# Down projection of a SwiGLU feed-forward layer: 16 of 22 depth tiles as seven half-width products

## The chip, the cores and the metric

The kernel runs on one core of one Trainium2 chip. The metric is the time of one execution on the device in microseconds. TensorE is the matrix engine, VectorE, ScalarE and GpSimd are the elementwise engines, SyncE issues the DMAs. In the profile they appear as PE (with PEld for its weight loads), DVE, ACT, POOL and SP.

## What is computed

The reference is one layer of a diffusion backbone: 512 latent tokens of width 1024 go through token mixers, then through a SwiGLU feed-forward layer of hidden width 2816 (22 tiles of 128), then through a final RMS norm. The change touches the end:

```python
def swiglu(h, w_gate, w_up, w_down):
    return (jax.nn.silu(h @ w_gate) * (h @ w_up)) @ w_down

# in reference():
h_lat = modulate(rms_norm(x, norm2_g[l]), mod_lat[3], mod_lat[4])
x = x + mod_lat[5] * swiglu(h_lat, ffn_w_gate[l], ffn_w_up[l], ffn_w_down[l])
...
return rms_norm(x, final_g)
```

`mod_lat[5]`, the gate of the residual, is one of six 1024-wide chunks of a projection of the conditioning vector.

## The kernel before

Everything lies transposed: a tile has 128 channels on its partitions and 512 tokens along its free axis. A product of weights and activations is done to nearly float32 accuracy by three matmuls: both operands are split into a rounded part `hi` and a rest `lo` (`split`, lines 128 to 130, and `load_unit`, lines 116 to 126: the cast on ScalarE, the subtraction on VectorE), and `mm3` (lines 132 to 137) adds hi x hi, hi x lo and lo x hi.

The feed-forward layer runs in two stages. In the gate and up stage each of 22 hidden tiles takes a gate and an up product of eight depth tiles. Four pairs are plain (`plain_pair`), 18 use `fast_pair` (lines 1094 to 1164): gate and up weights and the two token halves are the two-by-two blocks of a product that is formed from seven instead of eight half-width block products (Winograd's variant of Strassen's scheme). For that, VectorE makes four sums of weights for each pair (lines 1108 to 1112, `sa` and `sb`), and the sums of token halves are made once for the stage (`token_sums`). The seven products `p1` to `p7` have 12 matmuls each, of 256 columns. They come in two groups, `head` and `tail`: the tail of a pair is woven into the head of the next. Matmuls go in the order p1, p5 of the pair before, p7, p4 before, p6, p3 before, p2.

The down stage is plain: the 22 hidden tiles are split (loop over `hs`, lines 1187 to 1199, partly already during the gate and up stage), and each of eight output tiles takes three weight loads and 66 matmuls of 512 columns. `residual` (line 958) multiplies by the gate and adds into `x1`; squares are summed for the final norm. `ada(1)` loads one row block of the conditioning projection per output tile and makes a gate column from it on VectorE (line 861). The last output tile runs in two halves of 256 tokens, so that the norm and output of the first half run under the products of the second.

Raw weights pass through three buffers `wr` (`load_raw`, line 113), split ones through three pairs `whi` and `wlo`; within the fast pairs the split sums take four pairs `shi` and `slo`, the raw sums two buffers `S`. The order of the instructions on each engine is set ahead of time by a list scheduler from the program's order and its priorities (`tc.high_priority()` puts an instruction forward); at run time each engine works through its own queue in order. GpSimd's queue has memsets and eight elementwise products (line 795), all of them long before the feed-forward layer.

Of the kernel before, what the change touches and what calls it, by code (L numbers as in the profile page):

```python
# [12 lines left out]
P = 128  # L13
T = 512
# [38 lines left out]
def hybrid_block(ctx, tc, x, cx, cck, cc, wad, wada, vec, prm, cst, inv, win, wdt, wcv, wpl, wso, wout, wgu, wdn, out):  # L53
    nc = tc.nc

    class Ordered:
        def __init__(self, engine):
            self.engine = engine
# [31 lines left out]
    def vc(field, i, n=1):  # L90
        o = VEC_OFF[field] + i
        return vec_t[:, o : o + n]
# [856 lines left out]
    def project(o, ws, rhs, sl):  # L949
        n = sum(kn for _, kn in ws)  # L950
        q = 0
        for w, kn in ws:
            for k in range(kn):
                mm3(o[:, sl], w, k * P, tuple(a[:, sl] for a in rhs[q]), q == 0, q == n - 1)
                q += 1

    def residual(m, o, gate, base, sl, q, ms=None):
        V.scalar_tensor_tensor(x1[:, m, sl], o[:, sl], gate, base[:, sl], ALU.mult, ALU.add)
        if ms is None:
            sq_acc(acc[:, sl], x1[:, m, sl], m == 0, sl.stop - sl.start, q)  # L960
        else:
            S.activation(q[:, sl], x1[:, m, sl], AF.Square)
            PE.matmul(ms, mean, q[:, sl], start=False, stop=True)
# [80 lines left out]
    hid = []  # L1044

    def plain(u):
        if u < 3:
# [21 lines left out]
    def quad(tag, bufs, dt=F32):  # L1069
        return pt(f2, [P, 4, H], tag, bufs, dt)  # L1070
# [116 lines left out]
    hs = []  # L1187
    for q in range(NFF // 2):
        tags = ("shi", "slo") if q < 4 else ("T", "T") if q < 8 else ("S", "S") if q < 9 else None
        if tags:  # L1190
            pair = [pt(f2, [P, 2, T], tag, {"T": 8, "S": 2}.get(tag, 4), F32R) for tag in tags]
        for e in range(2):
            if tags:
                hi, lo = (a[:, e, :] for a in pair)
            else:
                hi, lo = (pt(per, [P, T], "hh", 8, F32R) for _ in range(2))
            split(hi, lo, hid[2 * q + e])
            hs.append((hi, lo))
    hid = hs

    acc = pt(per, [P, T], "sum", 1)
    for m in range(8):
        ada(1)
        o = mmp()
        ws = [(load_unit(wdn[m, :, k0 * P : (k0 + kn) * P], kn * P), kn) for k0, kn in ((0, 8), (8, 8), (16, 6))]
        for sl in halves if m == 7 else whole:
            ms = rms_head(sl) if m == 7 else None
            project(o, ws, hid, sl)
            residual(m, o, mod_l[:, 40 + m : 41 + m], x1[:, m, :], sl, pt(per, [P, T], "hl", 8), ms)
            S.activation(x1[:, m, sl], x1[:, m, sl], AF.Copy, scale=fin_n[:, m : m + 1])  # L1210
            if m < 7:
                continue
            rms_tail(ms, sl)
            n = T // 2
            for q in range(4):
                ot = pt(f2, [P, 2, n], "hid", NFF)
# [117 lines left out]
```

## Time and profile before

| | us |
|---|---|
| median of 3 runs | 976.66 (975.93 to 978.1) |
| profiled execution | 976.52 |
| its span, first to last instruction | 974.7 |
| TensorE busy in the span | 948.8 (97%) |
| VectorE busy | 764.9 (78%) |
| ScalarE busy | 492.2 (50%) |
| GpSimd busy | 15.9 (2%) |

The granted clock of TensorE is 0.996 of full speed over the span. The gate and up stage's fast pairs run from about 649 to 831 us, the down stage from 842 to 965, and the rest of 9.7 us is the second half's norm and output. A matmul's duration in the profile is longer than the distance to the next one, because matmuls overlap; what one costs is read from the distances.

### The profile page before, as it was taken

The page shows a single profiled execution, that of the slowest core. Times are in us where ns is not written, and L with a number is a line of the kernel's source. Part 1 is how long each engine was busy: PE and PEld are TensorE (multiplying, and loading weights), DVE is VectorE, ACT ScalarE, POOL GpSimd, SP SyncE. Part 2 cuts the span into 40 slices and gives each one's busy share as a digit, 9 for nine tenths or more (in the row PEclk, how much of TensorE's full clock was granted, in tenths as well). Part 3 has the DMA queues.
Part 4 walks back from the last instruction along what each step waited for, and adds up shares of the span by engine and source line. Part 5 has one row for each costly group of instructions (what it writes and reads, how often), then busy time and mean ns, then how long its engine had stood idle before and what let it go on. Part 6 is the DMA issues. An engine that isn't in the chain of part 4 may idle for free.

```text
span 974.7 us, 14173 instructions
## 1 busy us (share of the span) xinstructions
PE 948.8 (97%) x5420; PEld 803.6 (82%) x5420; DVE 764.9 (78%) x1165; ACT 492.2 (50%) x815; POOL 15.9 (2%) x58
## 2 busy tenths in 40 slices
PE   6999999999999999999999989999999999999996
PEld 4678888888887776777888769989999999888885
DVE  5589999967889999987876976999889888643333
ACT  5683597335445254644844434745555556432331
POOL 0000000000000000000000000000000000000000
PEclk9999999999999999999999999999999999999998
DMA  9753455321112346665578984223232323343422
GB/s 364 282 187 110 164 179 173 109 87 65 67 65 76 108 162 195 216 205 196 176 259 318 363 278 170 91 104 131 101 117 87 119 99 122 127 141 109 136 79 87
DMA packets 55492, 151.67 MB, mean 156 GB/s; under 512 B 5760, under 2 KB 16512, under 8 KB 54272
## 3 DMA queue, kind: packets, MB, share of 16 engines
q1 hardware_dynamic: 55424, 150.77, 44.6%
q8 instruction: 42, 0.69, 0.3%
q14 instruction: 26, 0.21, 0.1%
HBM read 134.43 MB, written 16.32 MB: 155 GB/s over the span
## 4 chain that ended last, share of the span: by engine, by line
PE 86%; DVE 7%; DMA 4%; ACT 2%; issue 1%; SPq 0%; DVEq 0%; ACTq 0%
PE mm L137 19%; PE mm L135 19%; PE mm L136 19%; PE mm L1122 10%; PE ps L1122 8%; PE mm L62 1%; DMA C<-mrg 1%; DVE wlo L123 1%; DVE A L403 1%; PE ps L1039 1%; PE ps L763 1%; PE y L825 1%; PE ps L62 1%; PE ps L715 1%; DMA wr<-in_wso_dram 1%
## 5 line engine op out<-in xcount | busy, mean ns | idle before, releaser
L135 PE MATMUL mm<-hh,whi 128*128 128x512 f32 (+1 forms) x612 | 242.4, 396 | 0.0
L137 PE MATMUL mm<-hh,wlo 128*128 128x512 f32 (+1 forms) x612 | 241.2, 394 | 0.5 <-DVE wlo L123 0.5
L136 PE MATMUL mm<-hl,whi 128*128 128x512 f32 x576 | 228.9, 397 | 0.0
L121 ACT CAST whi<-wr 128x1024 fp32r<-128x1024 f32 (+1 forms) x115 | 116.9, 1019 | 212.1 <-PE mm L136 167.4
L123 DVE TENSOR_TENSOR wlo<-wr,whi 128x1024 fp32r<-128x1024 f32 (+1 forms) x112 | 132.2, 1183 | 63.1 <-ACT whi L121 62.0
L137 PEld LDWEIGHTS mm<-hh,wlo 128*128 128x128 f32 x612 | 115.0, 188 | 28.3 <-issue 2.8
L135 PEld LDWEIGHTS mm<-hh,whi 128*128 128x128 f32 x612 | 115.1, 188 | 26.0 <-issue 1.7
L136 PEld LDWEIGHTS mm<-hl,whi 128*128 128x128 f32 x576 | 108.3, 188 | 25.0 <-issue 2.7
L403 DVE SCALAR_TENSOR_TENSOR A<-U,vec_t,A 128x504 f32<-128x504 f32 (+14 forms) x180 | 115.4, 684 | 0.1
L129 ACT CAST shi<-S 128x1024 fp32r<-128x1024 f32 x36 | 37.9, 1052 | 32.1 <-DVE S L1110 26.3
L1122 PE MATMUL mm<-T,shi 128*128 128x256 f32 x288 | 53.5, 283 | 0.0
L669 DVE SCALAR_TENSOR_TENSOR C<-C,vec_t,C 128x772 f32<-128x772 f32 (+1 forms) x48 | 46.9, 977 | 4.9 <-ACT C L667 2.4
L130 DVE TENSOR_TENSOR slo<-S,shi 128x1024 fp32r<-128x1024 f32 x36 | 44.1, 1225 | 5.8 <-ACT shi L129 5.7
L818 ACT ACTIVATE E<-E,sbias 128x128 f32<-128x128 f32 x128 | 40.0, 392 | 10.6 <-DMA E<-cumd 10.5
L1122 PEld LDWEIGHTS mm<-T,shi 128*128 128x128 f32 x288 | 44.8, 191 | 0.0
L129 ACT CAST whi<-wr 128x1024 fp32r<-128x1024 f32 (+1 forms) x36 | 30.0, 835 | 26.0 <-PE ps L1122 21.4
L861 DVE CUSTOM_DVE_ANT_0 wr<-wr,sil,vec_t 128x1024 f32<-128x1024 f32 x24 | 30.8, 1282 | 13.4 <-DMA wr<-in_wada_dram 13.4
L137 PE MATMUL mm<-H,wlo 128*128 128x256 f32 (+1 forms) x124 | 38.0, 307 | 2.9 <-DVE wlo L123 2.8
L1122 PE MATMUL mm<-T,slo 128*128 128x256 f32 x144 | 40.8, 284 | 0.0
L130 DVE TENSOR_TENSOR wlo<-wr,whi 128x1024 fp32r<-128x1024 f32 (+1 forms) x36 | 34.5, 958 | 7.6 <-ACT whi L129 6.0
L135 PE MATMUL mm<-H,whi 128*128 128x256 f32 (+1 forms) x124 | 37.8, 305 | 0.0
L136 PE MATMUL mm<-H,whi 128*128 128x256 f32 (+1 forms) x124 | 37.7, 304 | 0.0
(383 smaller groups left out, 2039.4 us busy)
## 6 DMA issues: line engine op xcount, KB each, us to landing
wr<-in_win_dram SPq DMA_DIRECT2D x62, 512.0 KB, 3.7
wr<-in_wgu_dram SPq DMA_DIRECT2D x44, 512.0 KB, 3.4
wr<-in_wada_dram SPq DMA_DIRECT2D x32, 512.0 KB, 4.0
E<-cumd SPq DMA_DIRECT2D x16, 512.0 KB, 5.3
wr<-in_wdn_dram SPq DMA_DIRECT2D x16, 512.0 KB, 3.9
X<-in_wad_dram SPq DMA_DIRECT2D x4, 1024.0 KB, 10.6
H<-in_wad_dram SPq DMA_DIRECT2D x4, 1024.0 KB, 11.2
mrg<-tmp SPq DMA_DIRECT2D x16, 256.0 KB, 4.0
```

What stands on the lines that cost most here:

```text
L121: S.copy(hi[:, :n], raw[:, :n])
L123: V.tensor_tensor(lo[:, :n], raw[:, :n], hi[:, :n], ALU.subtract)
L129: S.copy(dst_hi, src)
L130: V.tensor_tensor(dst_lo, src, dst_hi, ALU.subtract)
L135: PE.matmul(o, hi[:, col : col + P], rh, start=first, stop=False)
L136: PE.matmul(o, hi[:, col : col + P], rl, start=False, stop=False)
L137: PE.matmul(o, lo[:, col : col + P], rh, start=False, stop=last)
L403: V.scalar_tensor_tensor(accs[e][:, :, o], ins[e][:, :, q], vc("dw_w", (2 * j + e) * 31 + 15 + d), accs[e][:, :, o], ALU.mult, ALU.add)
L669: tap = V.scalar_tensor_tensor(a[:, 0:n], pad[:, k : n + k], vc("conv_w", i * 5 + k), a[:, 0:n], ALU.mult, ALU.add)
L818: S.activation(dec[d][:, j, :], dec[d][:, j, :], AF.Identity, bias=sbias[:, z, c : c + 1])
L861: V.tensor_tensor_reduce(raw, raw, silb[0], 1.0, vc("b_ada", i), ALU.mult, ALU.add, mod_l[:, i : i + 1])
L1122: PE.matmul(o[:, left], x[:, cs], rhs[k][y], start=first and k + n == 0, stop=k == 3 and n == 2, skip_group_check=True,)
```

## The change

The hidden tiles are kept in pairs. The first six of the 22 depth tiles are multiplied plainly: eight output tiles of 18 matmuls. The other 16 form two blocks of eight depth tiles. In a block, two output tiles (in the place of gate and up) and two token halves take the seven products of the fast pairs. Block 0 does all four pairs of output tiles, block 1 the first three; output tiles 6 and 7 of block 1 are plain, 24 matmuls each, tile 7 in two halves as before. Three contributions instead of one are added into `x1`. Each product leaves PSUM on its own: three by ScalarE with the gate as scale (`take`), four by VectorE with the gate and `x1` (`put`). GpSimd adds the first three into `x1` and makes the weight sums and the token sums. The gate columns are loaded and made during the six plain depth tiles, one for each output tile.

```diff
     def gated(up, sg):
-        h = pt(f2, [P, T], "hid", NFF)
+        if len(hid) % 2 == 0:
+            pairs.append(pt(f2, [P, 2, T], "hid", NFF // 2 + 1))
+        h = pairs[-1][:, len(hid) % 2, :]
         V.tensor_tensor(h, up, sg, ALU.mult)
...
-    adas.extend((5, q) for q in range(8))
+    gate_raw = deque()
+    def gate_load(m):
+        gate_raw.append(load_raw(wada[24 + m], 1024))
+    def gate_product(m):
+        raw, i = gate_raw.popleft(), 40 + m
+        V.tensor_tensor_reduce(raw, raw, silb[0], 1.0, vc("b_ada", i), ALU.mult, ALU.add, mod_l[:, i : i + 1])
...
+    gate_load(0)
     for i in range(NFF - PLAIN_TAIL, NFF):
         plain_pair(i)
...
+    KR = NFF - 16
+    down = []
+    for q in range(KR // 2):
+        hi, lo = (pt(f2, [P, 2, T], tag, 4, F32R) for tag in ("shi", "slo"))
+        split(hi, lo, pairs[q])
...
+    class Block:
...
+        def split_tile(self, hi, lo, sl):
+            k = len(self.x)
+            split(hi[:, sl], lo[:, sl], self.raw[k // 2][:, k % 2, sl])
+            self.x.append((hi, lo))
+        def token_sums(self):
+            for q in range(2):
+                a, b = (self.raw[q][:, :, sl] for sl in (left, right))
+                c, d = (self.raw[q + 2][:, :, sl] for sl in (left, right))
+                for dst, x, y in ((a, b, a), (b, d, b), (d, d, a), (c, c, d)):
+                    nc.gpsimd.tensor_tensor(dst, x, y, ALU.subtract)
+        def split_sum(self, n):
+            hi, lo = quad("T", 8, F32R), quad("T", 8, F32R)
+            base, sl = {1: (0, left), 3: (0, right), 2: (2, right), 4: (2, left)}[n]
+            for q in range(2):
+                es = slice(2 * q, 2 * q + 2)
+                split(hi[:, es, :], lo[:, es, :], self.raw[base + q][:, :, sl])
...
+    def down_pair(blk, j):
+        ks = slice(blk.k0 * P, (blk.k0 + 8) * P)
+        g, u = (load_raw(wdn[2 * j + e, :, ks], 1024) for e in range(2))
...
+        pool = nc.gpsimd.tensor_tensor
+        wa = parts(g, 1024)
+        pool(sa[:, c[0]], g[:, c[0]], u[:, c[0]], ALU.subtract)
+        pool(sb[:, c[0]], u[:, c[0]], u[:, c[1]], ALU.add)
+        pool(sa[:, c[1]], sb[:, c[0]], g[:, c[0]], ALU.subtract)
+        ws = parts(sa, 1024, 1)
+        pool(sb[:, c[1]], g[:, c[1]], sa[:, c[1]], ALU.subtract)
+        wu = parts(u[:, c[1]], T)
+        wt = parts(sb, 1024, 1)
...
+        def take(dst, o, gate):
+            with tc.high_priority():
+                S.activation(dst, o[:, left], AF.Copy, scale=gate)
+        def put(dst, o, gate):
+            with tc.high_priority():
+                V.scalar_tensor_tensor(dst, o[:, left], gate, dst, ALU.mult, ALU.add)
...
+        def p2():
+            product(b3, wa, T, blk.half(4, left), True)
+            put(x0[:, left], b3, g0)
+            pool(x0[:, left], x0[:, left], gt[:, left], ALU.add)
+            pool(x1u, x1u, ut, ALU.add)
+        def p5():
+            product(b1, wt, 0, blk.d[1], False)
+            put(x1u[:, right], b1, u0)
...
+        return (p1, p7, p6, p2), (p5, p4, p3)
...
     for m in range(8):
-        ada(1)
+        w = load_unit(wdn[m, :, 0 : KR * P], KR * P)
+        if m < 7:
+            gate_load(m + 1)
         o = mmp()
-        ws = [(load_unit(wdn[m, :, k0 * P : (k0 + kn) * P], kn * P), kn) for k0, kn in ((0, 8), (8, 8), (16, 6))]
+        project(o, [(w, KR)], down, whole[0])
+        gate_product(m)
+        add_down(m, o, whole[0])
+        if m in (2, 3, 4, 5):
+            b0.split_sum((3, 2, 1, 4)[m - 2])
+    jobs = [(b0, j) for j in range(4)] + [(b1, j) for j in range(3)]
+    tail = ()
+    for n, (blk, j) in enumerate(jobs):
+        head, nxt = down_pair(blk, j)
+        if n == 4:
+            b1.split_sum(3)
+            b1.split_sum(2)
+        for i in range(4):
+            head[i]()
+            if i < len(tail):
+                tail[i]()
+                if n == 4 and i < 2:
+                    b1.split_sum((1, 4)[i])
+        tail = nxt
+        if n < 3:
+            for _ in range((3, 3, 2)[n]):
+                a = pt(f2, [P, 2, T], "hid", NFF // 2 + 1, F32R)
+                b1.split_tile(a[:, 0, :], a[:, 1, :], whole[0])
+            if n == 2:
+                b1.token_sums()
+    ws = [load_unit(wdn[m, :, b1.k0 * P :]) for m in (6, 7)]
+    for f in tail:
+        f()
+    for m in (6, 7):
+        o = mmp()
         for sl in halves if m == 7 else whole:
             ms = rms_head(sl) if m == 7 else None
-            project(o, ws, hid, sl)
-            residual(m, o, mod_l[:, 40 + m : 41 + m], x1[:, m, :], sl, pt(per, [P, T], "hl", 8), ms)
-            S.activation(x1[:, m, sl], x1[:, m, sl], AF.Copy, scale=fin_n[:, m : m + 1])
+            project(o, [(ws[m - 6], 8)], b1.x, sl)
+            add_down(m, o, sl)
+            done(m, sl, ms)
```

`done` squares an output tile for the final norm and scales it, as before; `add_down` is the add from PSUM with the gate; `parts` splits a raw operand as in `fast_pair`.

## Rows read from the trace of the kernel before

**Rows 1.** Busy time by stretch: fast pairs, down stage (us, instructions; clock, DMA).

```profile
core 0: us, PE busy (x) PEld busy (x) DVE busy (x) ACT busy (x) POOL busy (x), PEclk, DMA share, GB/s
706.61:806.68 100.07, 100.07 (x843) 100.07 (x842) 86.07 (x121) 54.32 (x91) 0.00 (x0) 1.00 0.30 106
842.20:965.00 122.80, 122.65 (x600) 103.22 (x598) 45.63 (x57) 33.92 (x41) 0.00 (x0) 1.00 0.35 112
```

**Rows 2.** Chain of waits: start, duration (us), what; job starts, then successive output tiles.

```profile
706.61 2.86 PE mm L1122 x24
...
716.62 2.86 PE mm L1122 x24
...
736.63 2.86 PE mm L1122 x24
...
869.31 0.23 PE mm L135
...
884.37 0.24 PE mm L135
```

**Rows 3.** Timeline of VectorE, last output tile: start, duration (us), instruction, [idle before].

```profile
955.89 0.48 DVE L958 SCALAR_TENSOR_TENSOR X<-mm,mod_l,X 128x256 f32<-128x256 f32 x1 [6.29 <-PE mm L137]
...
960.56 2.50 DVE L1217 TENSOR_TENSOR hid<-X,sum 128x512 f32<-128x512 f32 x4
965.04 0.48 DVE L958 SCALAR_TENSOR_TENSOR X<-mm,mod_l,X 128x256 f32<-128x256 f32 x1 [1.98 <-PE mm L137]
967.27 0.43 DVE L143 TENSOR_TENSOR tmp<-tmp 128x256 f32<-128x256 f32 x1 [1.75 <-ACT tmp L141]
...
968.64 2.50 DVE L1217 TENSOR_TENSOR hid<-X,sum 128x512 f32<-128x512 f32 x4
```

**Rows 4.** Timeline of VectorE in the fast pairs, back-to-back instructions.

```profile
734.52 1.22 DVE L130 TENSOR_TENSOR wlo<-wr,whi 128x1024 fp32r<-128x1024 f32 x1
735.65 1.22 DVE L130 TENSOR_TENSOR slo<-S,shi 128x1024 fp32r<-128x1024 f32 x1
736.79 0.68 DVE L1055 TENSOR_TENSOR hid<-tmp,tmp 128x512 f32<-128x512 f32 x1
737.39 0.41 DVE L1145 TENSOR_TENSOR tmp<-tmp,ps 128x256 f32<-128x256 f32 x1
737.72 0.68 DVE L130 TENSOR_TENSOR wlo<-wr,whi 128x512 fp32r<-128x512 f32 x1
```

**Rows 5.** Instructions of one line: durations in ns (min/median/max), first and last start.

```profile
L795 POOL TENSOR_TENSOR W<-X,cbd x8: 1046/1158/2025, 326.9 to 445.2; 128x512 f32<-128x512 f32 x8
...
L820 DVE COPY_PREDICATED E<-msk,E x8: 1350/1390/2229, 130.1 to 427.0; 128x1024 f32<-128x1024 int32 x8
...
L403 DVE SCALAR_TENSOR_TENSOR A<-U,vec_t,A x4: 716/720/1511, 326.7 to 329.4; 128x488 f32<-128x488 f32 x4
```

**Rows 6.** Timeline of GpSimd and VectorE where a GpSimd product runs.

```profile
326.93 1.40 POOL L795 TENSOR_TENSOR W<-X,cbd 128x512 f32<-128x512 f32 x1 [37.37 <-DVE cbd L791]
...
353.33 1.27 POOL L795 TENSOR_TENSOR W<-X,cbd 128x512 f32<-128x512 f32 x1 [25.00 <-DVE cbd L791]
...
353.61 2.23 DVE L820 COPY_PREDICATED E<-msk,E 128x1024 f32<-128x1024 int32 x1
...
384.12 1.38 DVE L820 COPY_PREDICATED E<-msk,E 128x1024 f32<-128x1024 int32 x1
384.33 2.02 POOL L795 TENSOR_TENSOR W<-X,cbd 128x512 f32<-128x512 f32 x1 [29.73 <-issue]
```

**Rows 7.** Groups of VectorE in the down stage: count, busy us, mean ns, idle before.

```profile
L861 DVE CUSTOM_DVE_ANT_0 wr<-wr,sil_f,vec_t 128x1024 f32<-128x1024 f32 x6 | 7.7, 1285 | 21.6 <-DMA wr<-in_wada_dram 21.6
L123 DVE TENSOR_TENSOR wlo<-wr,whi 128x768 fp32r<-128x768 f32 x8 | 7.6, 950 | 0.0
L958 DVE SCALAR_TENSOR_TENSOR X<-mm,mod_l,X 128x512 f32<-128x512 f32 x7 | 5.3, 750 | 10.6 <-PE mm L137 10.6
...
L958 DVE SCALAR_TENSOR_TENSOR X<-mm,mod_l,X 128x256 f32<-128x256 f32 x2 | 1.0, 484 | 8.3 <-PE mm L137 8.3
```

**Rows 8.** DMA issues of the down stage: count, KB each, median us to landing.

```profile
wr<-in_wada_dram SPq DMA_DIRECT2D x7, 512.0 KB, 3.5
```

More of the change, by code (lines that the diff above doesn't have):

```diff
@@ L1042, in hybrid_block @@
                 PE.matmul(o[:, sl], lo[:, k * P : (k + 1) * P], h2[k][0][:, sl], start=False, stop=k == KT - 1)
-    hid = []
+    hid, pairs = [], []
     def plain(u):
@@ L1183, in hybrid_block @@
         f()
+    gate_load(0)
     for i in range(NFF - PLAIN_TAIL, NFF):
         plain_pair(i)
[L1187 to L1194, printed above, removed]
-            else:
-                hi, lo = (pt(per, [P, T], "hh", 8, F32R) for _ in range(2))
-            split(hi, lo, hid[2 * q + e])
-            hs.append((hi, lo))
@@ L1199, in hybrid_block, with __init__, half @@
-    hid = hs
-    acc = pt(per, [P, T], "sum", 1)
+    KR = NFF - 16
[3 more added lines that the diff above has]
+        split(hi, lo, pairs[q])
+        down += [(hi[:, e, :], lo[:, e, :]) for e in range(2)]
+    class Block:
+        def __init__(self, n):
+            self.k0 = KR + 8 * n
+            self.raw = pairs[self.k0 // 2 : self.k0 // 2 + 4]
+            self.x, self.d = [], {}
+        def split_tile(self, hi, lo, sl):
[14 more added lines that the diff above has]
+                split(hi[:, es, :], lo[:, es, :], self.raw[base + q][:, :, sl])
+            self.d[n] = [(hi[:, k, :], lo[:, k, :]) for k in range(4)]
+        def half(self, k0, sl):
+            return [tuple(a[:, sl] for a in self.x[k0 + k]) for k in range(4)]
@@ new lines, in down_pair, with parts, product, p1 @@
+    def down_pair(blk, j):
+        ks = slice(blk.k0 * P, (blk.k0 + 8) * P)
+        g, u = (load_raw(wdn[2 * j + e, :, ks], 1024) for e in range(2))
+        g0, u0 = (mod_l[:, 40 + 2 * j + e : 41 + 2 * j + e] for e in range(2))
+        x0, x1u = (x1[:, 2 * j + e, :] for e in range(2))
+        c = slice(0, T), slice(T, 2 * T)
+        sa, sb = pt(f2, [P, 2 * T], "S", 2), pt(f2, [P, 2 * T], "S", 2)
+        def parts(src, n, tag=None):
+            if tag is None:
+                hi, lo = pt(per, [P, 1024], "whi", 3, F32R), pt(per, [P, 1024], "wlo", 3, F32R)
+            else:
+                hi, lo = pt(f2, [P, 1024], "shi", 4, F32R), pt(f2, [P, 1024], "slo", 4, F32R)
+            split(hi[:, :n], lo[:, :n], src)
+            return hi, lo
+        pool = nc.gpsimd.tensor_tensor
[7 more added lines that the diff above has]
+        wt = parts(sb, 1024, 1)
+        b1, b2, b3 = mmp(), psp(), psp()
+        gt, ut = tmp(), tmp()
+        def product(o, w, base, rhs, first):
+            for k in range(4):
+                cs = slice(base + k * P, base + (k + 1) * P)
+                for n, (x, y) in enumerate(((w[0], 0), (w[0], 1), (w[1], 0))):
+                    PE.matmul(
+                        o[:, left], x[:, cs], rhs[k][y],
+                        start=first and k + n == 0, stop=k == 3 and n == 2, skip_group_check=True,
+                    )
+        def take(dst, o, gate):
[4 more added lines that the diff above has]
+                V.scalar_tensor_tensor(dst, o[:, left], gate, dst, ALU.mult, ALU.add)
+        def p1():
+            product(b1, wa, 0, blk.half(0, left), True)
+            take(gt[:, left], b1, g0)
+        def p7():
+            product(b2, ws, 0, blk.d[3], True)
+            take(ut[:, right], b2, u0)
+        def p6():
+            product(b1, ws, T, blk.d[2], False)
+            take(ut[:, left], b1, u0)
+        def p2():
[6 more added lines that the diff above has]
+            put(x1u[:, right], b1, u0)
+        def p4():
+            product(b2, wu, 0, blk.d[4], False)
+            put(x1u[:, left], b2, u0)
+        def p3():
+            product(b1, wt, T, blk.half(4, right), False)
+            put(x0[:, right], b1, g0)
+            if blk.k0 > KR:
+                done(2 * j, whole[0])
+                done(2 * j + 1, whole[0])
+        return (p1, p7, p6, p2), (p5, p4, p3)
@@ new lines, in hybrid_block, with done, add_down @@
+    acc = pt(per, [P, T], "sum", 1)
+    def done(m, sl, ms=None):
+        q = pt(per, [P, T], "hl", 8)
+        if ms is None:
+            sq_acc(acc[:, sl], x1[:, m, sl], m == 0, sl.stop - sl.start, q)
+        else:
+            S.activation(q[:, sl], x1[:, m, sl], AF.Square)
+            PE.matmul(ms, mean, q[:, sl], start=False, stop=True)
+        S.activation(x1[:, m, sl], x1[:, m, sl], AF.Copy, scale=fin_n[:, m : m + 1])
+    def add_down(m, o, sl):
+        V.scalar_tensor_tensor(x1[:, m, sl], o[:, sl], mod_l[:, 40 + m : 41 + m], x1[:, m, sl], ALU.mult, ALU.add)
@@ L1202, in hybrid_block @@
+    b0, b1 = Block(0), Block(1)
+    for k in range(8):
+        hi, lo = pt(per, [P, T], "hh", 8, F32R), pt(per, [P, T], "hl", 8, F32R)
+        b0.split_tile(hi, lo, left if k < 4 else whole[0])
+    b0.token_sums()
     for m in range(8):
-        ada(1)
+        w = load_unit(wdn[m, :, 0 : KR * P], KR * P)
+        if m < 7:
+            gate_load(m + 1)
         o = mmp()
-        ws = [(load_unit(wdn[m, :, k0 * P : (k0 + kn) * P], kn * P), kn) for k0, kn in ((0, 8), (8, 8), (16, 6))]
+        project(o, [(w, KR)], down, whole[0])
[3 more added lines that the diff above has]
+            b0.split_sum((3, 2, 1, 4)[m - 2])
@@ L1215, in hybrid_block @@
             for q in range(4):
-                ot = pt(f2, [P, 2, n], "hid", NFF)
+                ot = pt(f2, [P, 2, T], "hid", NFF // 2 + 1)[:, :, :n]
                 V.tensor_tensor(
```

## The prediction, made before the change was run

> **What bounds the kernel now.** I read the views in this order: busy time by stretch, the chain of waits, then the engine timelines of the three stages next to the change. The stretch of the down projection, 842.20 to 965.00, shows TensorE busy for 122.65 of 122.80 us at granted clock 1.00 (the 2.4 GHz level), VectorE for 45.63, ScalarE for 33.92 and GpSimd for nothing [rows 1]. So before the change this stage is TensorE alone, and a product less is time less. The stretch of the gate and up products, 706.61 to 806.68, is the nearest thing to what the change brings here: seven half-width products per pair, already in use there. TensorE is full there too, but VectorE stands at 86.07 of 100.07 us [rows 1]. In that stage GpSimd is idle as well, because VectorE makes the weight sums.
>
> The chain gives the two prices of TensorE. One job of 84 products of 256 columns runs from 706.61 to 716.62, 10.01 us, or 0.119 us each [rows 2]. One output tile of 66 products of 512 columns takes 869.31 to 884.37, 15.06 us, or 0.228 us each [rows 2]. Two half-width products thus cost 0.238 against 0.228, 4.5% more for the same columns.
>
> **What TensorE gains.** Before: seven tiles of 66 products of 512 columns and one tile in halves (132 of 256): 462 x 0.228 + 132 x 0.119 = 105.3 + 15.7 = 121.0 us; the other 1.8 of the 122.8 are the mean products and one short wait. After: 8 x 18 = 144 plain products of 512 (32.8 us), 7 jobs x 84 (70.1), tile 6 of the second block 24 of 512 (5.5), tile 7 in halves 48 of 256 (5.7): 114.1 us. The gain is 6.9 us if TensorE never waits.
>
> **The end.** Before, the first half's last product is out by 955.89 and the second's by 965.04, so the first half's chain (its four outputs from 960.56, 2.50 us) is finished under the second half's products [rows 3]. After, a half is 24 products, 2.9 us. With t0 the end of the first half, its outputs occupy VectorE from t0 + 4.7 to t0 + 7.1 (960.56 and 963.06 less 955.89) [rows 3]; the second half's chain is ready before that, and VectorE has the last 1.4 us of it (967.27 to 968.64) plus four outputs left to do: done at about t0 + 10.9. Before, from the second half's last product to its last output it took 6.1 us (965.04 to 968.64 + 2.50) [rows 3], which would be t0 + 9.0. The end costs 1.9 us if VectorE takes the second half's add first, 4.2 if that add stands behind the four outputs. I take 2.
>
> **What moves to GpSimd, and its price.** Per job four 128x512 weight sums go to GpSimd (on VectorE, 0.60 us from start to start [rows 4]), as well as two additions into x1 (one of 256 columns, one of 512). Each block adds eight 128x512 token sums. In units of 128x512: 7 x 4 + 7 x 1.5 + 2 x 8 = 54.5. The only such instruction in the trace is line 795, whose second operand is a small one; its shortest is 1.046 us, its median 1.158 [rows 5]. For a sum of two full operands, which the trace doesn't show, I take 1.05, as it passes as many elements; bounds are 0.68, what VectorE takes for one [rows 4], and 2.025, the longest [rows 5]. GpSimd's own load is 54.5 x 1.05 = 57 us, under the 103 us that TensorE needs from the first plain tile to the last job. That alone would be covered.
>
> What is not covered is what a GpSimd sum does to VectorE. Three of the eight tell it [rows 6]. At 384.33 the sum lasts 2.02 us: a COPY_PREDICATED with two SBUF inputs was running from 384.12, and the sum got its 1.05 us only behind it. At 353.33 the sum started 0.28 us before the next COPY_PREDICATED: that took 2.23 us, where its median is 1.390 [rows 5], so it was held for 0.84. At 326.93 the sum met back-to-back SCALAR_TENSOR_TENSORs of two SBUF inputs; one took 1.511 against 0.720 [rows 5]: held for 0.79. So a GpSimd sum and a VectorE instruction with two SBUF inputs take turns: a sum costs VectorE 0.8 us where one is due, and nothing where VectorE is idle or reads PSUM.
>
> The Trainium skill, "SBUF — State Buffer", section "Who interferes with whom", gives the rule: a VectorE instruction with two SBUF inputs and a GpSimd instruction that reads SBUF exclude each other, and the later one blocks until the first is through. The turns agree with the rows above; for the hold, the rule taken literally would give the whole sum, 1.05 us and not 0.8, and my sum below would be about 11 us longer.
>
> **VectorE's account, first plain tile to last job (103 us of TensorE).** Prices from start to start: 1.14 for 1024 columns, 0.60 for 512 and 0.33 for 256 [rows 4]; in the down stage I take 0.08 off the mean durations 0.950 (768 columns), 1.285 (gate column), 0.750 and 0.484 (add from PSUM) [rows 7]. Plain stage: six weight splits left 5.2, seven gate columns 8.4, eight adds 5.4, four token splits 2.4, eight split sums 4.8, the first job's three and a half weight splits 4.0: 30.2 us. Jobs: six more preparations 24.0, 28 adds from PSUM 11.2, second block's splits and split sums 9.6, four square sums 2.4, the two last weight splits 2.3: 49.5. Together 79.7 us, 77% of 103, less than the 86% that the gate and up stage bears without a wait of TensorE [rows 1].
>
> On top come the holds. At most 54.5 x 0.8 = 43.6 us, if every sum meets a two-input instruction; 16.6 us of VectorE's work reads PSUM and holds nobody. At best the sums fall into that and into VectorE's 23.3 idle us, and 3.7 us are left over. As the two-input part is 63.1 of 79.7 (79%), I take 43.6 x 0.79 = 34.4: VectorE would need 114.1 us for 103. Slack lets some of that pass, but the split of a job's first operand has little of it: in the gate and up stage one runs from 734.52 to 735.65 and its job starts at 736.63 [rows 2, 4]. A hold or two in front of it is enough for TensorE to wait. I take a delay of 11 us, most of it in jobs 2 to 4, where the second block's sums and splits (8 x 0.8 and 4.8 us) meet the running preparations. Ends: 0 (all covered) and 20 (every hold bites).
>
> **Other edits.** The gate columns now load one for each tile: two loads per 4.1 us of plain products on three raw buffers. A buffer is held for 3.5 us of transfer [rows 8] and some 2 of casts and splits, so three turn over twice in about 3.7 us: near the limit, but two tiles' weights are split ahead; I put 0 here, 3 us if VectorE's delay holds buffers longer. SP's queue is in order: behind a gate load that waits for a buffer stands the next tile's weight. GpSimd's add into x1 waits for the add from PSUM of the same job; behind it on GpSimd stand the next job's weight sums, and a later VectorE add waits for it. ScalarE keeps the casts and takes three scaled copies in place of plain ones; at 54.32 of 100.07 us in the like stage [rows 1] it covers the splits of the blocks. Pairs instead of single hidden tiles, and 12 fewer hidden splits in the gate and up stage, change nothing, as TensorE is full there.
>
> **The sum.** The profiled execution took 976.52 us, span 974.7, so 1.8 lie around it; the median shown is 976.66. Span: 974.7 - 6.9 (products) + 2 (end) + 11 (holds) = 980.8; time 982.6, say 982.5.
>
> **Rivals.**
> First, the holds are covered. The sums of a job come early in a period, when VectorE has little but adds from PSUM, and its big splits come late, after GpSimd is done; then the turns rarely collide. For it: 77% load; against it: the extra work of both blocks and the gate columns. Span 974.7 - 6.9 + 2 to 4 = 969.8 to 971.8, time 971.6 to 974, slightly faster.
> Second, every hold bites and VectorE's in-order queue adds idle time behind ScalarE's casts: delay 20 us and more, time 991.5 to 998. For it: each sum waits for VectorE in its turn (up to 0.97 us at 384.33 [rows 6]), and each chain of four sums with it; against it: PSUM adds free the port.
> Third, GpSimd's queue puts a job's x1 additions ahead of the next job's weight sums. They wait for the last product of the head; after it come 0.4 + 0.5 + 1.05, three sums 3.15, a cast of 1.05 and a split of 1.14 to the next job's second product, 7.3 us plus handovers where 2.9 are available: over 4.4 us in each of six jobs, 26 to 30 us, time about 1000. It decides as soon as those additions stand in front; against it speaks that VectorE's order in the like stage splits the next pair's sum (735.65) before it adds the running pair's last head product (737.39) [rows 4].
> Fourth, the change doesn't do what it says, because half-width products cost what they save. The measured 0.119 against 0.228 excludes more than the 4.5% counted above.
>
> **How the numbers follow.** Forecast (holds in part, 979 to 991): 0.53. Covered: 0.29. Every hold: 0.12. Queue order: 0.06. A measurement of this kernel can tell about 0.2%, 2 us. Faster by more: the covered case without its late end, 0.27. Within: the rest of it and the forecast's low end, 0.13. Slower: 0.60. The cases have both signs, so the range runs from the covered case to the second rival: 970.5 to 998; it leaves out the third rival and strays. The likeliest case's own range is 979 to 991.
>
> **What would show it.** In the profile after, the plain tiles should come 4.1 us apart and the jobs of the down stage more than 10.0 us apart, most of all jobs 2 to 4, with TensorE waiting for VectorE's splits; GpSimd sums longer than 1.05 us and VectorE's splits of 1024 columns longer than 1.23, side by side. Wrong would be jobs at 10.0 us throughout: then the holds cost nothing, and only the end is in question. Wrong on the other side would be TensorE waiting in every job for the second product behind GpSimd's additions.

## The result, and the profile after

The changed kernel took 1006.53 us (median of 4 runs, 1004.61 to 1007.19), the kernel before beside it 976.69 (4 runs, 975.93 to 978.1). The ratio is 1.0294, with a 95% interval of 1.0275 to 1.0312: 2.9% slower. The sign is the forecast one, but the time lies 24 us above the forecast and 8.5 above the end of its range.

The profiled execution took 1007.19 us, its span 1005.4, against 976.52 and 974.7 before. The page's line of busy times and two of its slice lines (the span in 40 slices):

```profile
PE 954.7 (95%) x5630; PEld 817.1 (81%) x5630; DVE 818.5 (81%) x1222; ACT 518.3 (52%) x863; POOL 99.5 (10%) x116
...
POOL 0000000000000001000000000000000005366540
PEclk9999999999999999999999999999999999979898
```

GpSimd's new work lies in the last quarter, and there the slices of TensorE's granted clock dip to 7 and 8 (0.982 over the span, 0.996 before). The busy times by stretch answer to [rows 1]. The stretches are the plain depth tiles, the seven jobs from the first start to the last, the rest of the products, and three short ones inside:

```profile
core 0: us, PE busy (x) PEld busy (x) DVE busy (x) ACT busy (x) POOL busy (x), PEclk, DMA share, GB/s
845.10:884.20 39.10, 35.19 (x146) 27.95 (x145) 37.52 (x41) 14.86 (x23) 21.93 (x14) 0.96 0.46 144
884.20:966.40 82.20, 64.26 (x470) 62.51 (x469) 45.33 (x54) 34.38 (x52) 50.24 (x38) 0.85 0.25 78
966.40:994.40 28.00, 27.55 (x200) 25.57 (x198) 14.90 (x23) 15.32 (x25) 5.65 (x4) 1.00 0.07 19
...
862.40:866.00 3.60, 3.52 (x9) 2.73 (x10) 3.60 (x7) 1.12 (x3) 0.00 (x0) 0.54 0.60 168
889.70:903.40 13.70, 4.92 (x25) 4.62 (x24) 6.41 (x6) 5.23 (x7) 6.01 (x6) 0.51 0.36 115
937.50:944.30 6.80, 5.88 (x27) 5.89 (x28) 6.61 (x8) 2.44 (x6) 3.76 (x3) 0.52 0.37 92
```

The line of the jobs says most of what there is to learn: in 82.20 us no engine is full. TensorE is busy for 64.26, VectorE for 45.33 (55%), GpSimd for 50.24 (61%), ScalarE for 34.38. In the plain stage VectorE is full (37.52 of 39.10), but that is not what TensorE waits for there, as the end of this section shows.

The span grew by 30.7 us, which adds up so:

| piece | us |
|---|---|
| the stage begins at 845.1 and not at 842.2 (code that the change doesn't touch; the fast pairs themselves began 3.3 later) | +2.9 |
| products saved, as worked out | -6.9 |
| plain depth tiles: 39.1, where 8 x 18 x 0.228 is 32.8 | +6.3 |
| first job start to last: 82.2, where 5.7 + 5 x 10.01 is 55.8 | +26.4 |
| rest of the products: one wait of 0.7 | +0.7 |
| from the last product to the end: 11.0 instead of 9.7 | +1.3 |

The job starts, to hold against [rows 2], are 884.18, 904.20, 914.89, 924.90, 936.65, 952.00 and 966.38. Job 0 took 20.0 us, the others 10.7, 10.0, 11.75, 15.35 and 14.4. TensorE's timeline shows its waits (start, duration, instruction, idle before it and what ended that):

```profile
860.76 0.50 PE L135 MATMUL mm<-shi,whi 128*128 128x512 f32 x1 [2.58 <-ACT whi L121]
...
887.65 0.51 PE L1266 MATMUL ps<-T,shi 128*128 128x256 f32 x2 [1.89 <-ACT shi L129]
...
899.32 0.80 PE L1266 MATMUL mm<-T,shi 128*128 128x256 f32 x2 [8.79 <-ACT tmp L1273]
...
936.65 0.50 PE L1266 MATMUL mm<-hid,whi 128*128 128x256 f32 x2 [1.51 <-ACT whi L129]
```

After such waits the clock is at its lower level: 0.51 to 0.54 of full speed (1.2 GHz) in the three short stretches above and in a fourth, 954.6 to 958.0 (3.00 us of products). TensorE was busy for 3.52 + 4.92 + 5.88 + 3.00 = 17.3 us in them; at the 2.4 GHz level half of that is enough, so at most 8.7 us of the loss is clock.

**The longest wait, step by step.** At about 890.5 TensorE needs the PSUM bank of job 0's first product, whose last matmul had started at 885.48. What empties it is a copy on ScalarE (line 1273). ScalarE's and GpSimd's timelines:

```profile
897.84 1.04 ACT L129 CAST shi<-S 128x1024 fp32r<-128x1024 f32 x1 [5.82 <-POOL S L1254]
898.79 0.47 ACT L1273 ACTIVATE tmp<-mm,mod_l 128x256 f32<-128x256 f32 x1
```

```profile
887.71 2.30 POOL L1256 TENSOR_TENSOR S<-wr,S 128x512 f32<-128x512 f32 x1
893.86 1.40 POOL L1252 TENSOR_TENSOR S<-wr,wr 128x512 f32<-128x512 f32 x1 [3.85 <-DMA wr<-in_wdn_dram]
895.21 1.26 POOL L1253 TENSOR_TENSOR S<-wr 128x512 f32<-128x512 f32 x1
896.55 1.26 POOL L1254 TENSOR_TENSOR S<-S,wr 128x512 f32<-128x512 f32 x1
```

The copy had nothing to wait for, but it stood in ScalarE's queue behind the cast of job 1's weight sum. That cast waited for three sums on GpSimd, these for a load, and the load for job 0's last sum (887.71 + 2.30), which gives the raw buffer back: 13 us of wait for a copy of 0.47.

**The ring.** From there on the chain of waits goes round. A piece of it, start and duration:

```profile
904.06 1.30 POOL S L1252
905.37 1.69 POOL S L1253
907.06 0.70 POOL X L1294
907.75 1.27 POOL S L1254
909.05 1.06 ACT shi L129
...
911.39 0.86 DVE X L1277 x2
912.25 1.14 DVE wlo L130
...
913.45 3.56 DMA wr<-in_wdn_dram
...
917.17 1.29 POOL S L1252
```

Three sums on GpSimd, the cast of the sum, its split on VectorE (910.13 to 911.35), two adds, the split of the first operand, which frees a raw buffer, the load into it, and the next job's first sum: 13.1 us once round, where TensorE needs 10.01 for a job.

**The turns.** VectorE and GpSimd hold each other up as [rows 6] said, and for longer. In the plain stage a gate column on VectorE lasts from 846.30 for 2.31 us (1.285 in [rows 7]); GpSimd's sum from 847.49 lasts 2.27:

```profile
846.30 2.31 DVE L1182 CUSTOM_DVE_ANT_0 wr<-wr,sil_f,vec_t 128x1024 f32<-128x1024 f32 x1
```

```profile
846.17 1.36 POOL L1221 TENSOR_TENSOR hid<-hid,hid 128x512 f32<-128x512 f32 x1
847.49 2.27 POOL L1221 TENSOR_TENSOR hid<-hid 128x512 f32<-128x512 f32 x1
```

An undisturbed sum lasts 1.26 to 1.30 (895.21 and 896.55 above, for instance). Over the stage the splits that took 950 ns in [rows 7] took 1269.

**The plain stage.** The wait at 860.76 is of the same kind as the longest one. ScalarE's timeline:

```profile
859.36 0.62 ACT L129 CAST T<-hid 128x512 fp32r<-128x512 f32 x1 [5.31 <-POOL hid L1221]
859.88 0.83 ACT L121 CAST whi<-wr 128x768 fp32r<-128x768 f32 x1
```

The weights that the second cast reads were loaded from 854.24 on and were there after 3.0 us, but the cast stood behind that of a token sum, for which ScalarE waited 5.31 us. That sum and the two before it on GpSimd lasted 1.64 to 1.88 us each (853.48 to 859.32), in turns with VectorE's splits. TensorE waited 2.58 us, then 0.98 for the split of the same weights, and its next 3.52 us of products were at the lower clock: together up to 5.3 of the 6.3 us that the stage lost.

### The profile page after: what moved, and what is told of

Same layout as the page of the kernel before. It is cut to its first block, busy times and chain, and to the rows that moved or that the text cites. A ratio compares the mean times of both kernels' runs of the same rounds, so it can differ in the third digit from the quotient of the medians.

```text
span 1005.4 us, 14806 instructions
## 1 busy us (share of the span) xinstructions
PE 954.7 (95%) x5630; PEld 817.1 (81%) x5630; DVE 818.5 (81%) x1222; ACT 518.3 (52%) x863; POOL 99.5 (10%) x116
## 5 line engine op out<-in xcount | busy, mean ns | idle before, releaser
L137 PE MATMUL mm<-hh,wlo 128*128 128x512 f32 x576 | 228.4, 397 | 0.7 <-DVE wlo L123 0.5
L135 PE MATMUL mm<-hh,whi 128*128 128x512 f32 x576 | 228.9, 397 | 0.0
L121 ACT CAST whi<-wr 128x1024 fp32r<-128x1024 f32 (+1 forms) x101 | 102.1, 1014 | 141.4 <-PE mm L136 93.9
L137 PEld LDWEIGHTS mm<-hh,wlo 128*128 128x128 f32 x576 | 108.3, 188 | 27.5 <-issue 2.8
L135 PEld LDWEIGHTS mm<-hh,whi 128*128 128x128 f32 x576 | 108.3, 188 | 24.8 <-issue 1.7
L130 DVE TENSOR_TENSOR slo<-S,shi 128x1024 fp32r<-128x1024 f32 x50 | 64.0, 1280 | 37.2 <-ACT shi L129 37.2
L129 ACT CAST shi<-S 128x1024 fp32r<-128x1024 f32 x50 | 52.5, 1050 | 70.9 <-POOL S L1254 37.7
L129 ACT CAST whi<-wr 128x1024 fp32r<-128x1024 f32 (+1 forms) x50 | 41.7, 834 | 32.4 <-PE ps L1124 23.0
L1221 POOL TENSOR_TENSOR hid<-hid 128x512 f32<-128x512 f32 x8 | 14.1, 1768 | 391.4 <-DVE hid L130 389.6
L818 ACT ACTIVATE E<-E,sbias 128x128 f32<-128x128 f32 x128 | 40.1, 393 | 13.1 <-DMA E<-cumd 13.0
L135 PE MATMUL mm<-H,whi 128*128 128x256 f32 (+1 forms) x124 | 37.8, 304 | 0.2 <-ACT whi L121 0.2
## 6 DMA issues: line engine op xcount, KB each, us to landing
X<-in_wad_dram SPq DMA_DIRECT2D x4, 1024.0 KB, 10.1
```

What stands on the lines that cost most here:

```text
L135: PE.matmul(o, hi[:, col : col + P], rh, start=first, stop=False)
L137: PE.matmul(o, lo[:, col : col + P], rh, start=False, stop=last)
L818: S.activation(dec[d][:, j, :], dec[d][:, j, :], AF.Identity, bias=sbias[:, z, c : c + 1])
```

## The experiments

Three accounts stood against each other, A, B and C in the expectations. **Turns** (A): the time goes where GpSimd's reads and VectorE's two-input instructions keep each other waiting. **Order** (B): GpSimd's sums are late, and what is queued in order behind their users is late with them. **The rest** (C): VectorE's work as a whole, or the products, the end and the gate columns, cost more than was counted. Each time stands beside runs of the kernel before on the same chip. On one chip these spread from 975.4 to 982.6 us, so a single run is good to some 4 us; times without a number of runs are single.

**The sums on VectorE.**

```diff
-        pool = nc.gpsimd.tensor_tensor
+        pool = V.tensor_tensor
...
-                    nc.gpsimd.tensor_tensor(dst, x, y, ALU.subtract)
+                    V.tensor_tensor(dst, x, y, ALU.subtract)
```

> All GpSimd sums (weight sums, token sums, additions into x1) made by VectorE, everything else as in the changed kernel. Theory A (turns: GpSimd's reads and VectorE's two-input instructions hold each other up): no holds are left, but VectorE then has 79.7 + 54.5 x 0.60 = 112 us of own work for 103 us of TensorE, so some 5 to 12 us stay lost: 975 to 983 us. Theory B (GpSimd's sums are merely late, and in-order queues turn that into waits of TensorE): the sums are early again, 970 to 976 us. Theory C (VectorE's total work is the bound wherever the sums are made): no better than the changed kernel, 1000 us or more.

Measured: 979.12 us (10 runs) against 978.88, ratio 1.0001 (0.9987 to 1.0016), no difference that can be measured. So the 30 us hang on where the sums run, and C falls as far as VectorE's work goes. The gain of the products doesn't show either: TensorE still waits about 1 us at several places while VectorE is busy for 120 of the 140 us from 842 to 982.

**Sums that only write, and no sums.** The first leaves the sums out but for four columns (two of each token half) and puts memsets of about the same time in their place, so GpSimd writes and hardly reads. The second leaves all sums out.

```diff
...
-        pool = nc.gpsimd.tensor_tensor
+        def pool(dst, x, y, op, n=2):
+            tiny = min(dst.shape[-1], 4)
+            nc.gpsimd.tensor_tensor(dst[:, 0:tiny], x[:, 0:tiny], y[:, 0:tiny], op)
+            for _ in range(n):
+                nc.gpsimd.memset(dst, 0.01)
...
```

```diff
-        pool(sa[:, c[0]], g[:, c[0]], u[:, c[0]], ALU.subtract)
...
-        ws = parts(sa, 1024, 1)
+        ws = parts(g, 1024, 1)
...
-        wt = parts(sb, 1024, 1)
+        wt = parts(u, 1024, 1)
```

> Each GpSimd sum is replaced by a sum of two to four columns (so that it still waits for the same operands) and by two or three memsets of its result, so that GpSimd is busy about as long in the same chain but hardly reads; the sums are left out, so the output is not the reference's. Theory A: nothing is left to take turns over, VectorE's splits go back to 1.23 us for 1024 columns, and the time falls to 973 to 985 us. Theory B: GpSimd's chain is as late as before, the time stays at 998 to 1007 us.

> All sums are left out (the splits of the weight sums take the raw weights, the token sums' splits the unsummed halves, the three scaled copies are not added), so the output is not the reference's. TensorE, ScalarE and the rest of VectorE have what they have in the changed kernel. Theories A and B: 970 to 975 us, the covered case. Theory C: the plain tiles and the jobs stay stretched, 985 us or more.

Measured: 985.09 and 974.14 us against 978.88. Without sums the jobs stand 10.0 us apart and the time falls by 4.7: as far as single runs can tell, products and end are priced right, and the third account falls. With writes alone most of the loss is gone, as the turns would have it, yet 11 us against no sums remain. VectorE's groups show splits that nothing disturbs, 1223 ns as in [rows 4], while GpSimd is busy for 74.87 of 140 us:

```profile
L1256 POOL MEMSET S<- 128x512 f32 x56 | 28.5, 525 | 1.6
...
L130 DVE TENSOR_TENSOR slo<-S,shi 128x1024 fp32r<-128x1024 f32 x14 | 17.1, 1223 | 24.5 <-ACT shi L129 24.5
```

The 24.5 us behind the bar are VectorE's idle time before those splits: sums that hold nobody are still late. So order costs something with hardly a turn.

**The copy ahead of the cast.** Aimed at the wait of 8.79 us (9.2 with a short one of its kind): ScalarE may issue a job's cast of the first sum only behind the last scaled copy that stands before it in the program (`takes` collects these copies).

```diff
...
+        with ExitStack() as st:
+            if takes:
+                st.enter_context(tc.issue_after(takes[-1].ins))
-        ws = parts(sa, 1024, 1)
+            ws = parts(sa, 1024, 1)
...
```

> Only ScalarE's order is mended: the cast of a job's first weight sum is queued behind the scaled copies of the head of the job before, so that a copy that frees a PSUM bank never stands behind a cast that waits for GpSimd. Theory B: the 9.2 us wait of TensorE in the first job goes, with the half clock behind it, 990 to 997 us. Theory A: the wait only moves to the next split that is late because of the holds, 1000 to 1007 us.

Measured: 999.14 us against 978.88, between the two expectations. That wait shrank to 2.1 us; the longest is now one of 3.95 us at 945.98, for a split on VectorE. The kernel gained 7 to 10 us against the changed one (1006.53 beside 976.69), and twenty remain. The gain is not that one wait's alone: the scheduler also gave at least ten instructions on VectorE another place in the queue.

**The same order, with writes alone.** The two edits above together.

> As e2 (GpSimd writes for as long, hardly reads; sums left out), with ScalarE's order mended as in e6. If the 11 us that e2 has over e3 come from ScalarE's copies that stand behind a cast that waits for GpSimd, 974 to 978 us. If they come from the splits that are late at their own matmuls, 981 to 986 us.

Measured: 973.66 us against 977.71, 4.1 below the kernel before: all of the loss is gone. On VectorE this kernel's queue differs from that of the last experiment by one swap of neighbours, on ScalarE by one swap and one cast that stands two places later, on GpSimd by one swap of token sums. Nor are the weight sums quicker: one of them takes 1.45 us from start to start (900.05 to 901.50), where an undisturbed one that reads takes 1.37 in the last experiment (906.35 to 907.72). What lies between the two (+20.3 and -4.1 against the kernel before, 24 us) is therefore the reading: the turns, with what they delay. One thing is not separated from it: a raw buffer is read by four columns alone, so GpSimd can be done with it some 1.1 us earlier. The stretches and groups of both, first with reads, then with writes:

```profile
842.00:982.00 140.00, 122.62 (x789) 110.88 (x789) 106.40 (x119) 62.88 (x95) 86.83 (x55) 0.95 0.31 93
...
L130 DVE TENSOR_TENSOR T<-hid,T 128x512 fp32r<-128x512 f32 x16 | 19.5, 1246 | 0.0
...
L1254 POOL TENSOR_TENSOR S<-wr,wr 128x512 f32<-128x512 f32 x7 | 12.0, 1711 | 6.5 <-DMA wr<-in_wdn_dram 4.7 <-DVE slo L130 1.7
```

```profile
842.00:960.00 118.00, 116.65 (x808) 108.55 (x807) 80.91 (x115) 64.36 (x98) 75.37 (x169) 1.00 0.35 106
...
L130 DVE TENSOR_TENSOR T<-hid,T 128x512 fp32r<-128x512 f32 x16 | 10.6, 685 | 0.4 <-ACT T L129 0.2
```

A sum that reads lasts 1711 ns in the mean of the job's first sums and not 1270, and a split of 512 columns 1246 ns and not 685: each pays for the other.

**Weight sums on GpSimd in the kernel before.** Its fast pairs make the same sums, on an otherwise idle GpSimd.

```diff
-        V.tensor_tensor(sa[:, c[0]], g[:, c[0]], u[:, c[0]], ALU.subtract)
+        nc.gpsimd.tensor_tensor(sa[:, c[0]], g[:, c[0]], u[:, c[0]], ALU.subtract)
```

and so for the other three of lines 1108 to 1112.

> The kernel before, with only the four weight sums of each fast pair of the gate and up stage moved from VectorE to GpSimd: 18 x 4 sums, no token sums, no additions, no blocks. If the turns cost what the changed kernel's trace shows (a sum of 1.25 us alone, 1.4 to 1.8 with its own waits), a job's port time is 4 x 1.25 + 4.0 = 9 of 10.0 us, and pairs go to 10.0 to 11 us each: 977 to 995 us. If steady jobs bear it, as jobs 1 to 3 of the changed kernel (10.0 to 10.7) suggest, 975 to 982 us. If every sum costs VectorE its whole length, over 1000 us.

Measured: 1014.38 us against 977.71, 37 us more. Over 1000 us was expected only if every sum cost VectorE its whole length. Yet there are hardly any turns: over the pairs the sums last 1.29 to 1.39 us in the mean of their lines and the splits 1.21 to 1.28. The chain shows the ring by itself:

```profile
742.30 4.34 DMA wr<-in_wgu_dram
...
746.80 1.29 POOL S L1108
...
749.42 1.30 POOL S L1110
...
750.75 1.06 ACT shi L129
...
753.50 1.15 DVE wlo L130
...
754.69 4.39 PE mm L1122 x22
```

From the issue of the load to TensorE, which waited for that last split, it takes 12.4 us for a pair of 10.01. The split of the sum runs from 751.83; the split of the first operand, which is due first and whose data had been there since 746.6, stands behind it in both queues.

**The first operand ahead.** The same kernel, with the cast and split of the sum issued only behind those of the first operand:

```diff
...
+        with tc.issue_after(last[0][0].ins), tc.issue_after(last[0][1].ins):
-        ws = parts(sa, 1024, 1)
+            ws = parts(sa, 1024, 1)
...
```

> As e7 (the kernel before, the fast pairs' weight sums on GpSimd), with one thing mended: the split of a pair's first weight sum is queued behind the split of its first operand, on ScalarE and on VectorE. In e7's trace a pair takes 12 us, sums last 1.29 us and splits 1.21, so hardly any turn collides; TensorE waits for the first operand's rest, which stands on VectorE behind a sum's split that waits for GpSimd. If the order of the queue is what costs there, pairs go to 10.0 to 10.8 us and the time to 977 to 990 us. If the chain of load, four sums, cast and split through three raw buffers sets 12 us by itself, it stays at 1005 us or more.

Measured: 983.37 us against 978.42. Of the 37 us, about 32 were the order of two queues. TensorE is busy for 169.53 of the 170 us from 660 to 830, although one of the four sums now meets a split each time and lasts 2184 ns:

```profile
L1110 POOL TENSOR_TENSOR S<-S,wr 128x512 f32<-128x512 f32 x18 | 39.3, 2184 | 1.4
```

So here turns cost little, and order nearly everything. The chain shows why: the cast and the splits no longer lie in the ring.

```profile
752.17 3.57 DMA wr<-in_wgu_dram
...
762.17 3.03 DMA wr<-in_wgu_dram
```

From one load to the next there is only the transfer and the pair's four sums, one of them with its turn: 10.00 us, just what a pair takes on TensorE.

**Which sums.** In the changed kernel: the weight sums on VectorE (GpSimd keeps token sums and additions); the token sums on VectorE (GpSimd keeps weight sums and additions); and the weight sums alone on GpSimd.

```diff
-        pool(sa[:, c[0]], g[:, c[0]], u[:, c[0]], ALU.subtract)
+        V.tensor_tensor(sa[:, c[0]], g[:, c[0]], u[:, c[0]], ALU.subtract)
...
```

```diff
-                    nc.gpsimd.tensor_tensor(dst, x, y, ALU.subtract)
+                    V.tensor_tensor(dst, x, y, ALU.subtract)
```

```diff
...
-            pool(x1u, x1u, ut, ALU.add)
+            V.tensor_tensor(x1u, x1u, ut, ALU.add)
```

(the first has the other three weight sums too, the third the other addition and the second's edit)

> The weight sums (28 of the 54.5 units) go back to VectorE, the token sums and the additions into x1 stay on GpSimd. By the holds alone, GpSimd's port time falls by half, and VectorE takes 16.8 us: 980 to 990 us. If the token sums of the first block, which lie in the plain stage, set the loss, 995 us or more.

> Only the token sums (16 of the 54.5 units) go back to VectorE; weight sums and additions into x1 stay on GpSimd. The plain stage's 6 us and half of the first job's 14 us should go, as the first block's sums lie there and the second block's stand among the first job's weight sums on GpSimd: 985 to 993 us. If the weight sums' lateness alone sets the loss, 998 us or more.

> Only the four weight sums of each job stay on GpSimd; the token sums and the two additions into x1 go to VectorE. The kernel with the weight sums and the additions on GpSimd took 1002.0 us, 23 us more than the kernel before beside it, its jobs 12 to 15 us apart. There the additions stand in GpSimd's queue ahead of weight sums of a later job and wait for the adds from PSUM. If that queue order is what holds the jobs, they come back to 10.0 to 10.7 us, and the time is 978 to 986 us. If it is the way of the weight sums themselves (load, three sums of 1.27 us, cast, split, buffer free again), the jobs stay 11 us and more apart, and the time is 992 to 1003 us.

Measured: 994.35 against 977.71, 1002.03 against 978.92, and 997.23 against 979.04. The first lies between its two expectations. The second lies 9 us above the range that was thought likely, and in the one for weight sums whose lateness alone sets the loss. Taking the token sums off GpSimd did mend the plain stage: it took 33.45 us (845.50 to 878.95) and not 39.10, without the wait of 2.58 us, although VectorE, which then makes these sums, was as full as before (32.17 us). But its jobs came 12.1 to 15.4 us apart. The third settles why: 28 weight sums alone, GpSimd busy for 40 of 140 us, nothing else in its queue, cost 18 us. Its chain from a load to TensorE:

```profile
931.04 3.44 DMA wr<-in_wdn_dram
934.64 2.16 POOL S L1252
...
938.13 1.29 POOL S L1254
939.44 1.06 ACT shi L129
940.53 1.33 DVE slo L130
941.86 1.14 DVE T L130 x2
...
944.66 1.15 DVE wlo L130
945.85 4.27 PE mm L1266 x22
```

It is the ring again, 14.8 us long, with one turn in it (2.16) and the splits of the second block. The jobs came 12.1 to 14.8 us apart.

**The gate columns off the stage.** If the sums have to stay on VectorE, other work can leave: the gate columns are made in the fast pairs, in buffers of hidden pairs that are free there. First in eight pairs in a row, loaded in the pair that uses them, then every second pair and loaded one ahead.

```diff
+        raw = pt(f2, [P, 2, T], "hid", NFF // 2 + 1).rearrange("p a b -> p (a b)")
+        nc.sync.dma_start(raw, wada[24 + m])
...
+        n = i - PLAIN_HEAD
+        if n < 16 and n % 2 == 0:
+            gate_load(n // 2)
+        elif n < 16:
+            gate_product(n // 2)
```

> As e1 (all sums on VectorE), but the eight gate columns are loaded into free hidden-pair buffers and made during fast pairs 2 to 9 of the gate and up stage, 8 x 1.2 = 9.6 us less for VectorE in the down stage. If e1 loses its 5 us to VectorE's load in the down stage, 973 to 977 us where e1 has 979, against 978.9 of the kernel before on that chip. If e1's loss comes from the order of the queues, no change from e1.

> As e8, but the gate columns are loaded one fast pair ahead and made in every second pair, so that no product waits for its transfer at the head of VectorE's queue. In e8 the jobs of the down stage take 10.0 us each and the fast pairs lose 4.4 us in one place, where VectorE waits 2.3 us for a gate column's transfer. If that is all, 971 to 974 us, 4 to 6 under the kernel before, the covered case of the prediction. If the gate columns are too much for VectorE in that stage, 975 to 978 us.

Measured: 976.71 us (10 runs), ratio 0.9982 (0.9971 to 0.9993); and 974.34 (6 runs) against 978.92, ratio 0.9953 (0.9936 to 0.9971). In the first the jobs were 10.0 us apart, but at one place a gate column waited 2.32 us for its load at the head of VectorE's queue, and the fast pairs took 186.4 us instead of 181.9. In the second they took 184.5, and it beats both kernels. From the first plain tile to the last job TensorE is full again, beside a VectorE that is 94% busy and has no partner to wait for:

```profile
838.00:954.00 116.00, 116.00 (x790) 108.00 (x789) 109.07 (x168) 64.36 (x101) 0.00 (x0) 1.00 0.30 90
```

## Why the prediction was right in sign and wrong in size

**Right: products and end.** Without sums the kernel is 4.7 us faster, with writes alone in a mended order 4.1: -6.9 for the products and some 2 for the end. The end went as worked out, VectorE taking the second half's add (994.68) ahead of the first half's outputs (995.53); it cost 1.3 us in the span against 2 in the sum. The price of the covered case, the first rival, was right, and its condition was not met.

**The step that failed: "I take a delay of 11 us".** It measured 6.3 + 26.4 + 0.7 = 33.4 us. The term came from an account of VectorE's time: 79.7 us of work and 34.4 of holds, 114.1 for 103. That is a test of throughput, and in the jobs throughput was not the limit: VectorE idled for 45% of that stretch. The same mistake stands in "That alone would be covered" about GpSimd's own 57 us under 103. It was not covered: with hardly a turn, four sums a pair cost the kernel before 37 us, and 28 weight sums cost the changed one 18. What counts is how long the way from a load to the next load is: in these queues 3.6 us of transfer, three sums, a cast, two splits. With sums of 0.60 us from start to start on VectorE that is 3.6 + 1.8 + 1.06 + 1.14 + 1.14 = 8.7, under 10.01; with 1.27 on GpSimd 10.8, over it, before anything else stands in between, and even with the prediction's 1.05 it is 10.1. These rows were at hand ([rows 4, 8], the cast of 1.05 in the third rival). Where the order took the cast and the splits out of that way, in the kernel before, 10.00 us were left, and the same sums cost 5 us and not 37.

**The price of a sum** was taken at 1.05 us, from instructions whose second operand is small. Two full operands took 1.26 to 1.30. In the ring's three sums that is 0.7 us per job.

**The hold** was taken at 0.8 us. The gate column shows 2.31 - 1.285 = 1.03. The Trainium skill, "SBUF — State Buffer", section "Who interferes with whom", has the later instruction blocked until the earlier is through, which for this sum would be up to 1.27; the gate column lies halfway between that and my 0.8. The Trainium skill also says there that a VectorE instruction with two SBUF inputs doesn't contend with a GpSimd instruction that only writes, and the run with memsets agrees: splits of 1223 ns beside a busy GpSimd.

**Raw buffers: "I put 0 here, 3 us if VectorE's delay holds buffers longer".** The load is a member of the ring: in the changed kernel the load that job 1's first sum waits for is issued at 890.03, when job 0's last sum is done, and in the piece of the ring above the load at 913.45 goes out when a late split lets go. A fourth raw buffer wasn't tried.

**Where it would show.** Named were jobs 2 to 4 and plain tiles 4.1 us apart. The plain tiles came 4.9 apart in the mean, but most of what they lost is one wait with the lower clock behind it, for a weight cast that stood on ScalarE behind a late token sum's cast. The prediction's "it covers the splits of the blocks", said of ScalarE from its busy time, failed there. That VectorE was full is not the cause: with the token sums on VectorE it was as full, and TensorE needed 33.45 us for the same tiles. The worst, counted from 0, were job 0 (20.0), which waits for its sums behind the token sums, and jobs 4 and 5 (11.75 was job 3, then 15.35 and 14.4), where the second block's splits lie in the ring.

**The rivals.** The second (every hold bites, 991.5 to 998) had the same account and fell short for the same reason. The third came nearest with its "about 1000", and its kind was right, one late producer and what stands in order behind it; its place was not. The additions into x1 do stand ahead of weight sums in GpSimd's queue, but ahead of those for the job after next, so that some 10 us are there and not 2.9. Taking them out of that queue gave some 5 of 23 us, little more than single runs can tell. The queues that cost most were ScalarE's (the copy and the weight cast behind casts of late sums) and, in the kernel before, those of the first operand behind the sum.

**The clock** was in no term. The four stretches at its lower level cost up to 8.7 us on top of the waits that they followed.

**What stays open.** Turns and order don't add up piece by piece: with ScalarE's order mended in the down stage the reading costs 24 us, and with the order mended in the kernel before the weight sums cost 5. Collisions are rarer there, and whether the 24 would shrink if the first operand went ahead in the changed kernel too was not run. How much of the 24 is the longer splits themselves and how much what they delay was not taken apart either. That unchanged code ran some 3 us later in the profiled execution is not explained either; the fast pairs began at 649.6 to 652.5 us in the experiments, at 648.8 in the kernel before.

## What to carry to other kernels

Before work moves to an idle engine, follow one buffer round from load to load, with the new engine's durations and everything that stands in order ahead of each step; if the round is longer than what the bounding engine needs, as here, the move can cost time though no engine is full. Sums on GpSimd and two-input instructions on VectorE also take turns, so that work which feeds VectorE's splits is better left there, and other work taken off VectorE (here the gate columns, into a stage with room). A producer that got slower should have its users queued behind everything that doesn't need it.

## What the runs showed of the hardware

A sum of two 128x512 float32 operands takes 1.26 to 1.30 us on GpSimd and 0.69 on VectorE (0.60 from start to start); a memset of that size takes 0.525 us on GpSimd and disturbs VectorE's splits by nothing that can be seen (1223 ns). A VectorE instruction of 1.285 us that reads two SBUF operands lasted 2.31 beside a sum, and the sum beside it 2.27. After TensorE's waits of 1 to 9 us the granted clock stood at 0.51 to 0.54 for the stretches shown.
